# A residual stage of a diffusion backbone: VectorE's work behind the first group's statistics is queued behind the root

## The chip, the cores and the metric

The kernel runs as one program on one core of a Trainium2 chip. The metric is the time of one execution in microseconds (us), the median of several runs. Four engines compute: TensorE (PE, matrix products), VectorE (DVE), ScalarE (ACT) and GpSimd (POOL); SyncE (SP) issues the DMAs. Each engine works through its own queue in order, and they wait for each other by semaphores.

## The reference

Two trunk layers are applied to 640 tokens: 512 latent tokens and 128 context tokens, which share the weights but have their own conditioning vector.

```python
def trunk_layer(x, cond, rope, ctx, layer_idx, ...):
    sh_a, sc_a, g_a, sh_f, sc_f, g_f = modulation(cond, w_mod, b_mod)
    h = rms_norm(x, norm_attn) * (1.0 + sc_a) + sh_a
    proj = h @ w_in
    ...                       # differential attention and grouped-query attention
    mix = jnp.concatenate([out_a, out_b], axis=-1) @ w_out
    x = x + g_a * mix
    h = rms_norm(x, norm_ffn) * (1.0 + sc_f) + sh_f
    gate, up = jnp.split(h @ w_gate_up, 2, axis=-1)
    x = x + g_f * ((jax.nn.silu(gate) * up) @ w_down)
    return x, own_ctx
```

`rms_norm` needs, for each token, the mean of the squares of all 1024 columns and the inverse root of it. So the next normalisation can only be finished when the last column of `x + g * (...)` is there. All values are 32-bit floats.

## The kernel before

The stream `x` is held with its columns in the 128 partitions: eight tiles `x0` to `x7` (`xT`) of 128 columns x 640 tokens (in the order of a built program they are named `x_70` to `x_77`). Every factor of a product is split into a high and a low part, `hi` and `lo` (for weights `whi` and `wlo`): ScalarE writes the high part (L87, or L90 with a bias), VectorE the low one (L88, L91), and `prod` (L710) makes three matmuls of it, high by high (L714), low by high (L715) and high by low (L716). Weights come by DMA into `raw`, and `w_prep` (L687) splits them some tiles ahead of use; `w_next(ahead)` says how many.

Three places close a sub-layer with the norm of the next one behind it, all by `residual` (L1168) with `nxt` given: attention to FFN in layer 0 (boundary 1), FFN of layer 0 to attention of layer 1 (boundary 2), attention to FFN in layer 1 (boundary 3). The first five column blocks go straight through: product into PSUM, `add_gated` (L1161, the gated sum into `x`; one instruction for latent, one for context tokens), `stat_add` (square on ScalarE L363, sum of squares on VectorE L364). For the last three, the tokens are taken in two groups: 256 and 384, or twice 320 at boundary 3. For each group in turn the three products, adds and statistics are made. Then `norm_stats` (L388) turns the sums into one number per token: PE sums over the partitions (L398), VectorE takes the inverse root in twelve small instructions that depend on each other (`rsqrt`, L99 to L105, the last writes `rstd`), and PE spreads `rstd` over the partitions (L402) into a PSUM tile `rb`. `norm_apply` multiplies `x` by the scale and by `rb` (L625, at boundary 3 L450) and splits the result; that is the input of the next products.

The source gives only dependencies and a priority by its order. The compiler's scheduler (`schedule_with_timeline_sim=True`) fixes each engine's queue by its own model of time: whatever it holds to be ready first goes first. So the twelve instructions of the first group's root may stand between instructions of the second group's adds and of the weight splits. PSUM tiles `S` (three of them) hold running products; a product can start when an earlier one's tile has been read.

Of the kernel before, what the change touches and what calls it, by code (L numbers as in the profile page):

```python
# [15 lines left out]
ALU = mybir.AluOpType  # L16
# [4 lines left out]
D = 1024  # L21
KC = D // P
# [24 lines left out]
class Net:  # L47
# [45 lines left out]
    def rsqrt(self, out, src, scale, n):  # L93

        v = self.nc.vector
        a = self.t([P, 32], "rs_a", bufs=2)[:, :n]
        b = self.t([P, 32], "rs_b", bufs=2)[:, :n]
        c = self.t([P, 32], "rs_c", bufs=2)[:, :n]
        v.tensor_scalar(a, src, scale, EPS, ALU.mult, ALU.add)  # L99
        v.tensor_scalar(b.bitcast(I32), a.bitcast(I32), 1, None, ALU.logical_shift_right)  # L100
        v.tensor_scalar(c.bitcast(I32), b.bitcast(I32), -1, 0x5F3759DF, ALU.mult, ALU.add)
        for i in range(3):
            v.scalar_tensor_tensor(b, c, -0.5, a, ALU.mult, ALU.mult)
            v.tensor_tensor(b, b, c, ALU.mult)
            v.scalar_tensor_tensor(out if i == 2 else c, b, 1.5, c, ALU.add, ALU.mult)  # L105


    def setup(self):
# [279 lines left out]
    def norm_stats(self, out, g0, g1):  # L388

        nc = self.nc
        st = self.mm()
        tiles = [(t, min(t, g1 - P)) for t in range(g0, g1, P)]
        n = len(tiles)
        for i, (_, s) in enumerate(tiles):
            nc.tensor.matmul(st[:, i:i + 1], lhsT=self.ssq[:, s:s + P], rhs=self.ones, start=True, stop=True)  # L398
        r = self.t([P, NTILE], "rstd", bufs=2)
        self.rsqrt(r[:, 0:n], st[:, 0:n], 1.0 / D, n)  # L400
        for i, (t, s) in enumerate(tiles):
            nc.tensor.matmul(out[:, t - g0:s + P - g0], lhsT=r[:, i:i + 1].broadcast_to([P, P]),  # L402
                             rhs=self.ident[:, t - s:P], start=True, stop=True)

    def norm_apply(self, state, group, rb):
        if state[1] and state[0] in FAST:
            self.fast_norm(state, group, rb)
            return
        g0, g1 = GROUPS[group]
        for k in range(KC):  # L410
            self.norm_chunk(state, k, g0, g1, rb)
# [756 lines left out]
    def residual(self, l, act, which, order, nxt=None, side=(), steps=1):  # L1168

        if nxt:
            self.stat_begin()
        for mb in range(KC - 3 if nxt else KC):
            w = self.w_next()
            s, parts = self.acc2()
            for i in range(2):
                self.prod(parts[i], self.columns(w, act, GROUPS[i], order))
            self.add_gated(l, which, mb, s, 0, NT)  # L1180
            if nxt:
                self.stat_add(mb, 0, NT)
                if mb == 2:
                    self.warm(AF.Silu if nxt[1] else AF.Exp)
            for _ in range(steps):
                self.step(side)
        if not nxt:
            return None
        while side:
            self.step(side)  # L1190
        state = self.norm_begin(*nxt)
        groups = HALVES if nxt[1] and nxt[0] in FAST else GROUPS
        last = [(mb, self.w_next(), self.acc2(groups)[1]) for mb in (KC - 3, KC - 2, KC - 1)]
        for i, (a, b) in enumerate(groups):
            for mb, w, parts in last:
                self.prod(parts[i], self.columns(w, act, (a, b), order))
                self.add_gated(l, which, mb, parts[i], a, b)
                self.stat_add(mb, a, b)
            rb = self.mm()
            self.norm_stats(rb, a, b)  # L1200
            self.norm_apply(state, i, rb)
        return state[2]

    def ffn(self, l, h, side):
# [135 lines left out]
```

## Time and profile before

| what | value |
|---|---|
| median of 3 runs | 1713.78 us (1711.89 to 1718.52) |
| profiled execution | 1714.41 us, span 1712.6 us |
| mean granted clock of TensorE | 0.984 of full speed |
| PE busy | 1655.6 us, 97% |
| DVE busy | 1173.0 us, 68% |
| ACT busy | 670.4 us, 39% |
| POOL busy | 436.7 us, 25% |

Busy shares are averages over the whole span. Idle time of PE is rare (the chain of work that ended last is 86% PE, 6% DVE, 3% DMA), so the places where PE stands still are worth looking at one by one, in the timeline of each engine. In it a row gives the start and the duration in us, the engine, the line, the operation, the tiles written and read, how many instructions were merged, and in brackets the idle time of the engine just before, with what ended it.

### The profile page before, as it was taken

Reading aid. Unit: us, or ns where it says so; the run is one execution under the profiler, and the core shown is the slowest. Engines: PE = TensorE matmul, PEld = TensorE weight load, DVE = VectorE, ACT = ScalarE, POOL = GpSimd, SP = SyncE. Lnnn points to the kernel's source line nnn. Section 1 sums busy time; section 2 is a strip of 40 time slices with the busy share of each in tenths; the row PEclk is TensorE's granted clock in tenths of the full one; section 3 lists DMA queues with packets and bytes.
Section 4 is the critical chain, followed back from the end, with each engine's and each line's share of the span. In section 5 each row is a group of like instructions: output and inputs, shape, how many; then the busy total and the mean of one; then the engine's idle time right before and its main releaser. Section 6 shows DMA issues by size and latency. Waiting matters only on the chain.

```text
span 1712.6 us, 29412 instructions
## 1 busy us (share of the span) xinstructions
PE 1655.6 (97%) x11958; PEld 1575.6 (92%) x11958; DVE 1173.0 (68%) x2023; ACT 670.4 (39%) x1301; POOL 436.7 (25%) x378
## 2 busy tenths in 40 slices
PE   8989899999999999999999998999999999999999
PEld 6768878898999999999998997888988999999998
DVE  5686768878488988732247885788479944973772
ACT  4433376643422122212235433767335422441440
POOL 0242634410100000000002354444013613641440
PEclk8989999999999999999999999999999999999999
DMA  9343211144155565412122212111311231231222
GB/s 348 120 153 118 56 26 26 50 173 148 50 181 189 177 217 170 151 50 99 56 86 89 83 32 50 26 38 47 115 50 47 77 104 70 74 112 62 74 82 79
DMA packets 44263, 169.22 MB, mean 99 GB/s; under 512 B 5600, under 2 KB 8416, under 8 KB 32864
## 3 DMA queue, kind: packets, MB, share of 16 engines
q1 hardware_dynamic: 44128, 167.34, 29.3%
q8 instruction: 94, 1.54, 0.4%
q14 instruction: 41, 0.34, 0.1%
HBM read 152.90 MB, written 3.93 MB: 92 GB/s over the span
## 4 chain that ended last, share of the span: by engine, by line
PE 86%; DVE 6%; DMA 3%; ACT 2%; POOL 2%; issue 1%; SPq 0%; DVEq 0%; POOLq 0%; ACTq 0%
PE S L715 21%; PE S L714 21%; PE S L716 21%; PE mm L1030 3%; PE S L1009 3%; PE S L925 3%; PE S L926 2%; PE mm L1026 2%; PE S L237 2%; PE mm L714 1%; PE mm L716 1%; PE mm L715 1%; DVE wlo L88 1%; DMA Q<-in_w_mod 1%; DMA raw<-in_w_in 1%
## 5 line engine op out<-in xcount | busy, mean ns | idle before, releaser
L87 ACT ACTIVATE whi<-raw 128x1024 fp32r<-128x1024 f32 (+2 forms) x272 | 225.0, 842 | 618.0 <-PE S L715 518.3
L88 DVE TENSOR_TENSOR wlo<-raw,whi 128x1024 fp32r<-128x1024 f32 (+2 forms) x272 | 293.7, 1093 | 96.6 <-ACT whi L87 92.1
L716 PE MATMUL S<-k,wlo 128*128 128x256 f32 (+2 forms) x904 | 280.1, 310 | 0.0
L714 PE MATMUL S<-k,whi 128*128 128x256 f32 (+2 forms) x904 | 277.7, 311 | 1.6 <-ACT k L90 1.2
L715 PE MATMUL S<-lo,whi 128*128 128x256 f32 (+2 forms) x880 | 272.4, 310 | 0.0
L716 PE MATMUL S<-hi,wlo 128*128 128x384 f32 (+2 forms) x864 | 266.9, 310 | 0.0
L714 PE MATMUL S<-hi,whi 128*128 128x256 f32 (+2 forms) x864 | 266.2, 310 | 0.0
L715 PE MATMUL S<-q,whi 128*128 128x256 f32 (+2 forms) x832 | 258.0, 310 | 0.0
L1161 DVE SCALAR_TENSOR_TENSOR x<-S,modT,x 128x128 f32<-128x128 f32 (+4 forms) x137 | 66.6, 524 | 195.5 <-PE S L716 195.4
L714 PEld LDWEIGHTS S<-k,whi 128*128 128x128 f32 x904 | 170.9, 190 | 3.2 <-ACT k L90 1.4
L716 PEld LDWEIGHTS S<-k,wlo 128*128 128x128 f32 x904 | 172.1, 190 | 0.0
L715 PEld LDWEIGHTS S<-lo,whi 128*128 128x128 f32 x880 | 165.4, 188 | 1.7 <-issue 1.7
L716 PEld LDWEIGHTS S<-hi,wlo 128*128 128x128 f32 x864 | 162.5, 188 | 0.0
L714 PEld LDWEIGHTS S<-hi,whi 128*128 128x128 f32 x864 | 161.7, 188 | 0.8 <-issue 0.8
L715 PEld LDWEIGHTS S<-q,whi 128*128 128x128 f32 x832 | 157.5, 189 | 3.4 <-issue 3.4
L317 DVE SCALAR_TENSOR_TENSOR Q<-V,cT,Q 128x512 f32<-128x512 f32 x224 | 152.6, 745 | 0.0
L714 PE MATMUL S<-whi,hi 128*128 128x256 f32 x512 | 147.1, 288 | 2.4 <-ACT Q L245 1.9
L632 POOL TENSOR_TENSOR lo<-P,hi 128x640 fp32r<-128x640 f32 (+2 forms) x12 | 13.3, 1107 | 533.8 <-ACT hi L631 533.4
L945 DVE TENSOR_REDUCE mx<-S 128x1 f32<-128x768 f32 x128 | 119.5, 951 | 43.4 <-PE S L926 43.1
L716 PE MATMUL S<-whi,lo 128*128 128x256 f32 x512 | 146.2, 286 | 0.2 <-DVE lo L91 0.2
L715 PE MATMUL S<-wlo,hi 128*128 128x256 f32 x512 | 145.7, 285 | 0.0
L714 PEld LDWEIGHTS S<-whi,hi 128*128 128x128 f32 x512 | 97.9, 191 | 5.5 <-issue 2.5
(272 smaller groups left out, 3632.5 us busy)
## 6 DMA issues: line engine op xcount, KB each, us to landing
raw<-in_w_gate_up SPq DMA_DIRECT2D x44, 1024.0 KB, 4.8
V<-in_w_mod SPq DMA_DIRECT2D x64, 512.0 KB, 3.9
raw<-in_w_in SPq DMA_DIRECT2D x16, 1024.0 KB, 4.8
raw<-in_w_down SPq DMA_DIRECT2D x16, 1024.0 KB, 5.0
Q<-in_w_mod SPq DMA_DIRECT2D x32, 256.0 KB, 3.8
raw<-in_w_out SPq DMA_DIRECT2D x8, 1024.0 KB, 4.9
raw<-in_w_down SPq DMA_DIRECT2D x8, 768.0 KB, 4.2
raw<-raw SPq DMA_DIRECT2D x40, 128.0 KB, 2.2
```

Source lines behind the costliest of these rows:

```text
L87: nc.scalar.activation(hi, src, AF.Copy)
L88: nc.vector.tensor_tensor(lo, src, hi.bitcast(F32), ALU.subtract)
L237: nc.tensor.matmul(o, lhsT=l_[k][:, c], rhs=r_[:, w], start=k == 0 and i == 0, stop=k == KC - 1 and i == 2)
L317: ins = nc.vector.scalar_tensor_tensor(a, v, self.cT[:, k, c:c + 1], a, ALU.mult, ALU.add)
L714: self.nc.tensor.matmul(out, lhsT=lh, rhs=rh, start=(i == 0), stop=False)
L715: self.nc.tensor.matmul(out, lhsT=lh, rhs=rl, start=False, stop=False)
L716: self.nc.tensor.matmul(out, lhsT=ll, rhs=rh, start=False, stop=(i == n - 1))
L925: nc.tensor.matmul(out, lhsT=Q[j][:, cols], rhs=keys[:, k0:k0 + n], start=True, stop=False)
L945: nc.vector.tensor_reduce(mx, s[:, 0:n], AX.X, ALU.max, negate=True)
L1009: nc.tensor.transpose(ps[:, i * P:(i + 1) * P], p[:, i * P:(i + 1) * P], self.ident)
L1030: nc.tensor.matmul(o[64 * j:64 * j + 64], lhsT=self.V[:, v, 512 + 64 * j:576 + 64 * j], rhs=pts[j][:, i * P:(i + 1) * P], start=first, sto ...
L1161: self.nc.vector.scalar_tensor_tensor(x[:, s:e], src[:, s - a:e - a], self.m(l, which, mb, c), x[:, s:e], ALU.mult, ALU.add)
```

## The change

`rsqrt` and `norm_stats` return the last instruction of the root. In `residual`, the loop over the two groups is taken apart: the first group is finished, then everything that VectorE gets from `norm_apply` of the first group, from the whole second group (adds, statistics, root) and from one more weight tile is queued behind the last instruction of the first group's root. `issue_after` sets an order in VectorE's queue; it adds no wait for a result. The last `w_next` prepares one tile less ahead, and `w_prep` inside the block makes up for it. In the changed kernel L364 is L365, L398 and L402 are L399 and L403, L450 is L452, L625 is L627 and L1161 is L1163.

```diff
-            v.scalar_tensor_tensor(out if i == 2 else c, b, 1.5, c, ALU.add, ALU.mult)
+            ins = v.scalar_tensor_tensor(out if i == 2 else c, b, 1.5, c, ALU.add, ALU.mult)
+        return ins.ins
...
-        self.rsqrt(r[:, 0:n], st[:, 0:n], 1.0 / D, n)
+        ins = self.rsqrt(r[:, 0:n], st[:, 0:n], 1.0 / D, n)
         for i, (t, s) in enumerate(tiles):
             nc.tensor.matmul(out[:, t - g0:s + P - g0], lhsT=r[:, i:i + 1].broadcast_to([P, P]),
                              rhs=self.ident[:, t - s:P], start=True, stop=True)
+        return ins
...
-        last = [(mb, self.w_next(), self.acc2(groups)[1]) for mb in (KC - 3, KC - 2, KC - 1)]
-        for i, (a, b) in enumerate(groups):
+        last = [(mb, self.w_next(1 if mb == KC - 1 else 2), self.acc2(groups)[1]) for mb in (KC - 3, KC - 2, KC - 1)]
+
+        def finish(i):
+            a, b = groups[i]
             for mb, w, parts in last:
                 self.prod(parts[i], self.columns(w, act, (a, b), order))
                 self.add_gated(l, which, mb, parts[i], a, b)
                 self.stat_add(mb, a, b)
             rb = self.mm()
-            self.norm_stats(rb, a, b)
-            self.norm_apply(state, i, rb)
+            return rb, self.norm_stats(rb, a, b)
+
+
+        rb, chain = finish(0)
+        with self.tc.issue_after(chain):
+            self.norm_apply(state, 0, rb)
+            rb, _ = finish(1)
+            self.w_prep(self.pos + 2)
+        self.norm_apply(state, 1, rb)
         return state[2]
```

What the scheduler makes of it, at boundary 1 on VectorE. `x_75` to `x_77` are the last three column blocks, `PT` the sums of squares, `wlo` a weight's low part, `A` the scale. Before:

```order
L99 TENSOR_SCALAR rs_a<-mm 128x2
L385 SCALAR_TENSOR_TENSOR A<-modT,small 128x8
L88 TENSOR_TENSOR wlo<-raw,whi 128x1024
L385 SCALAR_TENSOR_TENSOR A<-modT,small 128x8
L100 TENSOR_SCALAR rs_b<-rs_a 128x2
L364 TENSOR_TENSOR PT<-PT 128x384
L101 TENSOR_SCALAR rs_c<-rs_b 128x2
...
L105 SCALAR_TENSOR_TENSOR rstd<-rs_b,rs_c 128x2
L625 SCALAR_TENSOR_TENSOR P<-x_70,A,mm 128x256
```

Now, from the start of the root on:

```order
L99 TENSOR_SCALAR rs_a<-mm 128x2
L100 TENSOR_SCALAR rs_b<-rs_a 128x2
L101 TENSOR_SCALAR rs_c<-rs_b 128x2
...
L105 SCALAR_TENSOR_TENSOR rstd<-rs_b,rs_c 128x2
L1163 SCALAR_TENSOR_TENSOR x_75<-S,modT,x_75 128x256
L1163 SCALAR_TENSOR_TENSOR x_75<-S,modT,x_75 128x128
L1163 SCALAR_TENSOR_TENSOR x_76<-S,modT,x_76 128x256
L1163 SCALAR_TENSOR_TENSOR x_76<-S,modT,x_76 128x128
L1163 SCALAR_TENSOR_TENSOR x_77<-S,modT,x_77 128x256
L1163 SCALAR_TENSOR_TENSOR x_77<-S,modT,x_77 128x128
L88 TENSOR_TENSOR wlo<-raw,whi 128x1024 x3
L627 SCALAR_TENSOR_TENSOR P<-x_70,A,mm 128x256
```

The root is in one piece, both scale instructions are ahead of it, and the six adds and three splits, which stood ahead of the root or between its parts, are between it and the first multiplication of `norm_apply`.

At boundary 1 on TensorE, around the second group's broadcast; `k_44..` and `q_44..` are high and low parts of the FFN's input. Before:

```order
L714 MATMUL S<-k_4409,whi 128x256
L402 MATMUL mm<-ident,rstd 128x128 x3
L715 MATMUL S<-q_4417,whi 128x256
L716 MATMUL S<-k_4409,wlo 128x256
L714 MATMUL S<-k_4410,whi 128x256
```

Now:

```order
L717 MATMUL S<-q_4418,whi 128x256
L718 MATMUL S<-k_4410,wlo 128x256
L403 MATMUL mm<-ident,rstd 128x128 x3
L716 MATMUL S<-k_4403,whi 128x384 x3
L717 MATMUL S<-q_4411,whi 128x384
```

The broadcast stood among products of the first group (256 tokens); now it stands behind the last of them and directly ahead of the first product of the second group (384 tokens), which needs it.

At boundary 2 on VectorE, behind the first group's root; `lo_88..` are low parts of the projection's input. Before:

```order
L105 SCALAR_TENSOR_TENSOR rstd<-rs_b,rs_c 128x2
L364 TENSOR_TENSOR PT<-PT 128x384
L625 SCALAR_TENSOR_TENSOR P<-x_70,A,mm 128x256
L625 SCALAR_TENSOR_TENSOR P<-x_71,A,mm 128x256
L625 SCALAR_TENSOR_TENSOR P<-x_72,A,mm 128x256
L99 TENSOR_SCALAR rs_a<-mm 128x3
L91 SCALAR_TENSOR_TENSOR lo_8821<-P,modT,hi_8813 128x256
```

Now:

```order
L88 TENSOR_TENSOR wlo<-raw,whi 128x1024 x2
L365 TENSOR_TENSOR PT<-PT 128x384
L1163 SCALAR_TENSOR_TENSOR x_77<-S,modT,x_77 128x256
L1163 SCALAR_TENSOR_TENSOR x_77<-S,modT,x_77 128x128
L627 SCALAR_TENSOR_TENSOR P<-x_70,A,mm 128x256
L627 SCALAR_TENSOR_TENSOR P<-x_71,A,mm 128x256
L627 SCALAR_TENSOR_TENSOR P<-x_72,A,mm 128x256
L88 TENSOR_TENSOR wlo<-raw,whi 128x1024
L365 TENSOR_TENSOR PT<-PT 128x384
L91 SCALAR_TENSOR_TENSOR lo_8821<-P,modT,hi_8813 128x256
```

Ahead of these rows stand `rstd` and the adds to `x_75` and `x_76`. So two pairs of adds, two splits, a statistics add and a third pair are between `rstd` and the first multiplication, and one more split and statistics add between the multiplications and the first low part.

## Rows read from the trace of the kernel before

**Rows 1.** The page, first part: busy time and share of each engine.
```profile
PE 1655.6 (97%) x11958; PEld 1575.6 (92%) x11958; DVE 1173.0 (68%) x2023; ACT 670.4 (39%) x1301; POOL 436.7 (25%) x378
```

**Rows 2.** PE's waits: who for whom, us in total, times, longest.
```profile
PE mm L402 <- DVE rstd L105: 6.3, 2, 4.0
```

**Rows 3.** Timeline of PE at boundary 1: start, duration, row, idle before.
```profile
421.74 0.92 PE L402 MATMUL mm<-ident,rstd 128*128 128x128 f32 x4 [4.03 <-DVE rstd L105]
422.45 1.28 PE L398 MATMUL mm<-ones,PT 128*128 128x1 f32 x6
423.77 1.00 PE L714 MATMUL S<-k,whi 128*128 128x256 f32 x3
...
431.13 0.83 PE L402 MATMUL mm<-ident,rstd 128*128 128x128 f32 x6
...
435.34 0.69 PE L714 MATMUL S<-k,whi 128*128 128x384 f32 x3
```

**Rows 4.** Timeline of DVE at boundary 1.
```profile
411.56 0.74 DVE L1161 SCALAR_TENSOR_TENSOR x<-S,modT,x 128x256 f32<-128x256 f32 x2 [1.75 <-PE S L716]
412.48 1.23 DVE L88 TENSOR_TENSOR wlo<-raw,whi 128x1024 fp32r<-128x1024 f32 x1 [0.17 <-ACT whi L87]
...
417.78 0.15 DVE L99 TENSOR_SCALAR rs_a<-mm 128x2 f32<-128x2 f32 x1
...
419.87 0.16 DVE L103 SCALAR_TENSOR_TENSOR rs_b<-rs_c,rs_a 128x2 f32<-128x2 f32 x1
...
421.43 0.16 DVE L105 SCALAR_TENSOR_TENSOR rstd<-rs_b,rs_c 128x2 f32<-128x2 f32 x1
422.69 1.26 DVE L625 SCALAR_TENSOR_TENSOR P<-x,A,mm 128x256 f32<-128x256 f32 x3 [1.10 <-PE mm L402]
...
432.08 2.04 DVE L625 SCALAR_TENSOR_TENSOR P<-x,A,mm 128x256 f32<-128x256 f32 x6 [2.20 <-PE mm L402]
434.04 1.14 DVE L91 SCALAR_TENSOR_TENSOR q<-P,modT,k 128x256 fp32r<-128x256 f32 x3
```

**Rows 5.** Timeline of ACT behind boundary 1.
```profile
432.60 0.80 ACT L90 ACTIVATE k<-P,modT 128x256 fp32r<-128x256 f32 x2 [2.81 <-DVE P L625]
...
446.31 1.06 ACT L87 ACTIVATE whi<-raw 128x1024 fp32r<-128x1024 f32 x1 [5.14 <-PE S L715]
447.27 0.68 ACT L1237 ACTIVATE P<-S 128x640 f32<-128x640 f32 x1
```

**Rows 6.** Windows: length; busy PE, PEld, DVE, ACT, POOL; PEclk, DMA share, GB/s.
```profile
423.80:428.80 5.00, 5.00 (x23) 5.00 (x24) 4.97 (x18) 3.81 (x9) 2.01 (x3) 0.50 0.01 2
...
1275.30:1278.50 3.20, 3.20 (x12) 3.20 (x13) 3.06 (x13) 1.13 (x2) 0.00 (x0) 0.51 0.02 5
```

**Rows 7.** Timeline of PE at boundary 2.
```profile
904.46 0.71 PE L402 MATMUL mm<-ident,rstd 128*128 128x128 f32 x4 [2.30 <-DVE rstd L105]
...
906.99 0.58 PE L716 MATMUL S<-whi,lo 128*128 128x256 f32 x1 [0.20 <-DVE lo L91]
```

**Rows 8.** Timeline of DVE at boundary 2.
```profile
897.54 0.55 DVE L364 TENSOR_TENSOR PT<-PT 128x384 f32<-128x384 f32 x1
898.01 0.15 DVE L99 TENSOR_SCALAR rs_a<-mm 128x2 f32<-128x2 f32 x1
...
905.21 1.26 DVE L625 SCALAR_TENSOR_TENSOR P<-x,A,mm 128x256 f32<-128x256 f32 x3 [0.34 <-PE mm L402]
...
906.46 0.48 DVE L91 SCALAR_TENSOR_TENSOR lo<-P,modT,hi 128x256 fp32r<-128x256 f32 x1
```

**Rows 9.** Timeline of PE at boundary 3.
```profile
1273.66 0.42 PE L715 MATMUL S<-k,whi 128*128 128x320 f32 x1 [1.10 <-DVE k L91]
...
1275.28 0.57 PE L715 MATMUL S<-k,whi 128*128 128x320 f32 x1 [0.47 <-DVE k L91]
...
1280.15 0.78 PE L402 MATMUL mm<-ident,rstd 128*128 128x128 f32 x6
```

**Rows 10.** Timeline of DVE at boundary 3.
```profile
1272.17 0.97 DVE L100 TENSOR_SCALAR rs_b<-rs_a 128x3 int32<-128x3 int32 x1
```

## The prediction

> **What bounds the kernel now.** The page's first part comes first: TensorE (PE) is busy 97% of the span [rows 1], so a microsecond counts only where PE stands still, or runs at its lower clock. The view of PE's waits comes next: the longest wait for VectorE (DVE) in the whole kernel is that of the broadcast at L402 for `rstd`, 6.3 us in two places [rows 2]. The timeline then puts these at the two boundaries of layer 0: 4.03 us before 421.74 (boundary 1, attention to FFN) [rows 3] and 2.30 us before 904.46 (boundary 2, FFN to layer 1) [rows 7]. At boundary 3 (layer 1, attention to FFN) there is no such row; PE reaches L402 there without waiting for the root. The reader is to see in rows 3 and 4 what ends the stop: the root's twelve instructions run from 417.78 to 421.43+0.16, L402 follows at 421.74, DVE takes its result at 422.69, and PE's first product starts at 423.77, 1.08 us after that. After it the clock is at 0.50 for 5 us [rows 6].
>
> **Boundary 1, part by part.** *The root.* Undisturbed it needs 0.195 us a step (419.87 to 421.43 is eight steps) [rows 4], so twelve instructions last 11 x 0.195 + 0.16 = 2.3 us instead of 3.8, because a split of weights and a statistics add leave it. One small scale instruction now stands before it (+0.1). So `rstd` ends at 417.78 + 0.1 + 2.3 = 420.2, 1.4 us earlier, and L402 with it.
>
> *What the root displaced.* The order shows what now stands between `rstd` and the first L627 (L625 before): the gated adds of the last three column blocks and the low halves of three weight tiles. Before, all adds and two splits ran from 407 on, in time in which DVE waited for PE (1.75 us of idle before 411.56 alone) [rows 4]; now they run after 420.2. A pair of adds takes 0.74 and a split 1.23, each less the 0.08 by which neighbours overlap: 3 x 0.66 + 3 x 1.15 = 5.4 us. The first L627 starts at 425.6 instead of 422.69: **+2.9**. The cover is only the 1.10 us in which DVE waited for L402 anyway [rows 4], and it is in this sum. PE's first product follows 1.08 later, at 426.7.
>
> *The statistics of the second group.* Their L398 took 1.28 us in the stop, between 422.45 and 423.77 [rows 3]. Now it stands among products, because the adds and squares that it needs are late. At full clock I take 0.7 for it, and 0.3 for the first low half (L91), which has a statistics add more before it: **+1.0**.
>
> *The second broadcast.* Before, L402 of the second group was issued at 431.13 in the middle of first-group products, and PE worked on these until the second group's first product at 435.34 [rows 3]; DVE (432.08) and ScalarE (432.60) made that group's input meanwhile [rows 4, 5]. In the new order L403 stands behind all products of the first group. PE then has nothing: from L402's start to the first high half ready it is 432.60 + 0.80 - 431.13 = 2.27 us, of which L402 itself fills 0.7, so 1.6 stand open; the first low half (434.04 + 0.75) comes 1.4 us after that, of which the three products that need the high half alone fill 0.5. **+2.5**.
>
> *The next accumulator.* The three running products now end within 1 us of each other, and the fourth needs the bank of the first. ScalarE puts a split of 1.06 before the Silu of 0.68 that frees it [rows 5]; 1.7 less that 1 us of work: **+0.9**, the slack of the last term being read off the new order, so 0 to 1.7.
>
> *The clock.* The stop before the first product is now 5.8 us in place of 4.03 (and the 1.28 in which only L398 ran), and a second one of 2.5 us is added. After the first, PE again runs at the lower clock (0.50) for a stretch; I take the same cost as before. For the second, boundary 3 gives the nearest rows: stops of 1.10 and 0.47 us before 1273.66 and 1275.28 [rows 9] were followed by 3.2 us at 0.51 [rows 6], in which half the speed costs 1.6 us: **+1.6**, bounds 0 and 5 (both stretches twice as long).
>
> The Trainium skill (TensorE: Matmul & The Clock Gate, section "Why this matters for your kernels") warns that an idle gap between bursts of matmuls puts the array back to half rate. The rows agree that a stop is followed by 0.50, and by that rule this change, which makes a longer stop and one more, would lose at the clock again, as the last term has it; without the rule's second fall the sum below would be 1.6 less.
>
> Boundary 1 together: 2.9 + 1.0 + 2.5 + 0.9 + 1.6 = **8.9 us** (5 to 13).
>
> **Boundary 2.** The root starts at 898.01 at the latest and lasts 2.3, so `rstd` is there at 900.3, while PE has products until 904.46 - 2.30 = 902.16: PE's wait for the root is gone, 2.3 us. But DVE has two pairs of adds, two splits, a statistics add (0.55 less 0.08) and the third pair to do first [rows 4, 8]: 900.3 + 3 x 0.66 + 2 x 1.15 + 0.5 = 905.0, against 905.21 for the first L625. So the first product gains 0.2. Then the third split and another add (1.15 + 0.5) stand before the first L91, which was at 906.46 and comes at 905.0 + 3 x 0.4 + 1.6 = 907.8; PE waited for that L91 already, before 906.99 [rows 7], and now does so 1.3 us longer. The second group's L398 adds 0.4 to it, half of what it took among products above, as PE also waited in places there. **+1.7** (0 to 3).
>
> **Boundary 3.** The root already lay beside products; nothing is gained. The first L91 moves by a few tenths. The second group's root, until now interleaved with L450 and L91, is queued behind them as a block; one of its instructions also ran long (L100 0.97, where a step of the root is 0.195) [rows 10]. It ends about 0.3 us after 1280.15, where L402 started without a wait [rows 9], and PE, whose input came no later, stands still before it in one piece (some 2.9 us) and not in two (1.10 and 0.47 before). I take 0.3 and 1.3 for a lower clock after it, from the 1.6 above: **+1.6** (0 to 3.5).
>
> GpSimd's work shared that time. The Trainium skill (SBUF — State Buffer, section "Who interferes with whom") says that a GpSimd instruction and a VectorE one that takes the shared port pair exclude each other; the long L100 fits it. By it the block of twelve, if it meets GpSimd's instructions as they start later, could lose another 2 us, and the sum would be 14; otherwise it stays.
>
> **Sum.** 8.9 + 1.7 + 1.6 = 12.2 us on the profiled execution of 1714.41: 1726.6. That execution is 0.6 above the median of the runs shown (1713.78), so the median to expect is **1726**. The other small shifts of the order (in layer 1's projection and attention) I take at nothing: the same instructions stand there a place or two apart, beside PE's work; uncovered they could be half a microsecond either way. Bounds added up: 5 + 0 + 0 to 13 + 3 + 3.5, that is 1719 to 1733.
>
> **Rivals.** *No change (within 0.5%, 1705 to 1722).* The second stop is covered and the fourth accumulator comes in time, so boundary 1 pays only 2.9 + 1.0, boundary 2 1.3 and boundary 3 0.3: 5.5 us, 1719. For it: terms of 2.5 and 0.9 rest on the place of L403 in a queue, and on products that PE at half clock would do more slowly, giving DVE time. Against: L403 stands behind all of them, however slow they are. *Faster.* What the root no longer waits for decides, and the displaced work fits in the time of L402: boundary 1 gains 1.4 and boundary 2 2.3, and with shorter stops the clock stays up, worth at most 2.5 (half of 5 us at 0.50) and 2.8 more: 9 us, 1705. For it: `rstd` is what the view of waits names. It decides if less than 1.1 us of DVE work stands between `rstd` and L627; the order has 5.4 and 4.7 there, so hardly. *It doesn't do what it says* is excluded by the order: the root stands as one block at all three places.
>
> **Chances.** Forecast (slower by 12, beyond 0.5%): 0.80. No change: 0.17. Faster: 0.03. 0.5%, 8.6 us, is about what a measurement of this kernel can tell from no change. The range 1718 to 1733 holds the forecast's bounds and the upper part of the second case.
>
> **What would show it.** Right: at boundary 1, `rstd` near 420.2, the first L627 near 425.6, PE's first product near 426.7, a new stop of 2 to 3 us right behind the second group's L403 and the second group's first product near 440; at boundary 2, L403 near 902 without a wait for `rstd`, and the first L91 near 907.8. Wrong: if the first product at boundary 1 comes before 424, the displaced work was not on the path; if the second stop is missing, the sum is too high by 2.5 to 4.

## The result and the profile after

The changed kernel takes 1727.19 us (median of six runs, 1725.16 to 1730.47) against 1713.34 (1709.44 to 1718.52) of the kernel before: the ratio is 1.0085, with a 95% interval of 1.0071 to 1.0099. It is slower by 12 to 17 us; 1726 had been forecast. The profiled execution lasts 1727.22, with a span of 1725.3. The first part of the page, beside [rows 1]: PE has as much to do as before, and the span is 12.7 us longer.

```profile
PE 1655.9 (96%) x11958; PEld 1575.9 (91%) x11958; DVE 1177.6 (68%) x2023; ACT 671.6 (39%) x1301; POOL 438.6 (25%) x378
```

PE's waits in the changed kernel (for whom; us in total, times, longest), beside [rows 2]. In the new program the three matmuls of `prod` are L716 to L718; in e4, e7 and e9 further down some lines have moved by one more.

```profile
PE S L716 <- ACT k L90: 7.7, 3, 5.0
...
PE S L883 <- DVE Q L859: 5.3, 3, 2.4
...
PE S L716 <- ACT hi L90: 3.6, 2, 3.1
...
PE mm L403 <- DVE rstd L105: 3.2, 2, 2.5
```

The wait for `rstd` has fallen from 6.3 to 3.2 us, as the change intends. In its place stand waits of the first products for their input (k and hi), which the kernel before did not show with such lengths.

Boundary 1 on PE, which answers to [rows 3] (start, duration, row, idle before):

```profile
418.30 0.50 PE L399 MATMUL mm<-ones,PT 128*128 128x1 f32 x4
421.33 1.17 PE L403 MATMUL mm<-ident,rstd 128*128 128x128 f32 x4 [2.53 <-DVE rstd L105]
427.52 1.01 PE L716 MATMUL S<-k,whi 128*128 128x256 f32 x3 [5.03 <-ACT k L90]
434.06 0.72 PE L399 MATMUL mm<-ones,PT 128*128 128x1 f32 x6
438.86 0.83 PE L403 MATMUL mm<-ident,rstd 128*128 128x128 f32 x6
441.17 0.79 PE L716 MATMUL S<-k,whi 128*128 128x384 f32 x3 [1.49 <-ACT k L90]
442.56 0.44 PE L717 MATMUL S<-q,whi 128*128 128x384 f32 x1 [0.59 <-DVE q L91]
...
455.51 0.38 PE L716 MATMUL S<-k,whi 128*128 128x256 f32 x1 [0.70 <-ACT P L1248]
```

And on DVE, which answers to [rows 4]:

```profile
421.02 0.16 DVE L105 SCALAR_TENSOR_TENSOR rstd<-rs_b,rs_c 128x2 f32<-128x2 f32 x1
421.10 2.04 DVE L1163 SCALAR_TENSOR_TENSOR x<-S,modT,x 128x256 f32<-128x256 f32 x6
423.05 3.49 DVE L88 TENSOR_TENSOR wlo<-raw,whi 128x1024 fp32r<-128x1024 f32 x3
426.45 1.26 DVE L627 SCALAR_TENSOR_TENSOR P<-x,A,mm 128x256 f32<-128x256 f32 x3
```

This execution came to the boundary 1.09 us later than that of before, by chance (the program up to there is unchanged). With that taken off, `rstd` starts at 419.93 and not at 421.43, but between it and the first multiplication lie 5.4 us of adds and splits. The multiplication starts at 425.36 in place of 422.69, PE's first product at 426.43 in place of 423.77. Behind the second broadcast (438.86) PE stands still twice, for 1.49 and 0.59 us; it had worked on there before.

Boundary 2 on PE and DVE, beside [rows 7] and [rows 8] (this execution is 7.50 us later here):

```profile
909.50 0.61 PE L403 MATMUL mm<-ident,rstd 128*128 128x128 f32 x4
913.25 0.58 PE L716 MATMUL S<-whi,hi 128*128 128x256 f32 x1 [3.14 <-ACT hi L90]
915.95 0.58 PE L718 MATMUL S<-whi,lo 128*128 128x256 f32 x1 [1.91 <-DVE lo L91]
...
917.70 1.41 PE L399 MATMUL mm<-ones,PT 128*128 128x1 f32 x6
...
926.83 0.39 PE L716 MATMUL S<-whi,hi 128*128 128x256 f32 x1 [0.48 <-ACT hi L90]
```

```profile
912.18 1.26 DVE L627 SCALAR_TENSOR_TENSOR P<-x,A,mm 128x256 f32<-128x256 f32 x3
...
914.95 1.34 DVE L91 SCALAR_TENSOR_TENSOR lo<-P,modT,hi 128x256 fp32r<-128x256 f32 x2
```

Where the time went can be read by pairing each product of PE with the same product in the first trace of before and watching how the difference of their starts grows. It grows in five places; the columns are the differences over each stretch, in us, for the traces of all experiments below (b. 1 is boundary 1).

```
                            start   b. 1   b. 2  projection  attention  b. 3   all
changed kernel               1.1    6.4    2.5     2.3         1.3      -0.9   12.7
changed again (e10)         -0.4    6.3    2.5     2.3         1.2      -1.0   11.0
before again (e11)          -0.4   -0.5   -0.3    -0.2         0.4      -1.2   -2.1
e1 boundary 1 only           1.8    8.4    0.0    -0.2        -1.0      -0.9    8.1
e2 boundary 2 only           1.8   -0.4    2.7     2.3         1.4      -0.9    6.9
e3 boundary 3 only           1.6   -0.7   -0.5    -0.2        -0.5      -1.2   -1.3
e4 statistics early         -1.1    2.2    0.1     2.3         0.3       1.1    4.8
e5 adds only                 0.0    2.8   -0.1     0.0         0.3      -1.1    2.0
e6 splits only               0.2    0.5   -0.3     0.2        -0.4      -1.0   -0.7
e7 multiplications first     1.4    9.4   -0.1     0.1         0.2      -1.1    9.8
e8 b. 2, head root whole    -1.8    0.0    3.1     1.1         1.7      -0.9    3.1
e9 second broadcast ahead   -0.5    5.7   -0.4    -0.2        -0.4      -1.1    3.1
e12 products in the stop     2.3   -1.2   -0.3     0.1        -0.6      -1.2   -0.9
```

The first column is chance alone, up to four us between executions of the same instructions, and single traces have to be held against it. So have those rows of the other columns in which the order was the old one: they lie between -0.7 and 0.0 at boundary 1, and between -1.0 and 0.4 in the attention.

### The profile page after: what moved, and what is told of

The parts are those of the page before. It is cut to its first block, busy times and chain, and to the rows that moved or that the text cites. A ratio compares the mean times of both kernels' runs of the same rounds, so it can differ in the third digit from the quotient of the medians.

```text
span 1725.3 us, 29404 instructions
## 1 busy us (share of the span) xinstructions
PE 1655.9 (96%) x11958; PEld 1575.9 (91%) x11958; DVE 1177.6 (68%) x2023; ACT 671.6 (39%) x1301; POOL 438.6 (25%) x378
## 5 line engine op out<-in xcount | busy, mean ns | idle before, releaser
L716 PE MATMUL S<-k,whi 128*128 128x256 f32 (+2 forms) x904 | 277.3, 310 | 8.6 <-ACT k L90 7.7
L718 PE MATMUL S<-k,wlo 128*128 128x256 f32 (+2 forms) x904 | 278.7, 309 | 0.0
L718 PE MATMUL S<-hi,wlo 128*128 128x384 f32 (+2 forms) x864 | 267.0, 310 | 0.0
L716 PE MATMUL S<-hi,whi 128*128 128x256 f32 (+2 forms) x864 | 266.2, 310 | 0.0
L1163 DVE SCALAR_TENSOR_TENSOR x<-S,modT,x 128x128 f32<-128x128 f32 (+4 forms) x137 | 66.2, 525 | 186.4 <-PE S L718 186.2
L716 PEld LDWEIGHTS S<-k,whi 128*128 128x128 f32 x904 | 170.3, 189 | 10.8 <-ACT k L90 8.4
L718 PEld LDWEIGHTS S<-k,wlo 128*128 128x128 f32 x904 | 170.7, 189 | 0.0
L718 PEld LDWEIGHTS S<-hi,wlo 128*128 128x128 f32 x864 | 162.5, 188 | 0.0
L716 PEld LDWEIGHTS S<-hi,whi 128*128 128x128 f32 x864 | 161.7, 188 | 0.8 <-issue 0.8
L716 PE MATMUL S<-whi,hi 128*128 128x256 f32 x512 | 148.4, 290 | 5.7 <-ACT hi L90 3.6
L634 POOL TENSOR_TENSOR lo<-P,hi 128x640 fp32r<-128x640 f32 (+2 forms) x12 | 13.9, 1162 | 536.8 <-ACT hi L633 534.3
L718 PE MATMUL S<-whi,lo 128*128 128x256 f32 x512 | 146.6, 287 | 1.9 <-DVE lo L91 1.9
L716 PEld LDWEIGHTS S<-whi,hi 128*128 128x128 f32 x512 | 99.3, 194 | 9.1 <-ACT hi L90 4.0
```

The source lines that it names most:

```text
L716: self.nc.tensor.matmul(out, lhsT=lh, rhs=rh, start=(i == 0), stop=False)
L718: self.nc.tensor.matmul(out, lhsT=ll, rhs=rh, start=False, stop=(i == n - 1))
L1163: self.nc.vector.scalar_tensor_tensor(x[:, s:e], src[:, s - a:e - a], self.m(l, which, mb, c), x[:, s:e], ALU.mult, ALU.add)
```

## The experiments

Each experiment edits the part of `residual` behind `norm_begin`, or one other place. Their runs of the kernel before have medians of 1713.65 (e1 to e4), 1713.44 (e5 to e8) and 1713.52 (e9 to e12). Each of these three sets ran on a chip of its own, so versions of different sets are compared with care.

### One boundary at a time

The whole new block of `residual` is used at one boundary, the old loop at the others (e2 has `(1, 0)` in the condition, e3 `(1, 1)`):

```
+        if nxt == (0, 1):
             last = [(mb, self.w_next(1 if mb == KC - 1 else 2), self.acc2(groups)[1]) for mb in (KC - 3, KC - 2, KC - 1)]
...
+        else:
+            last = [(mb, self.w_next(), self.acc2(groups)[1]) for mb in (KC - 3, KC - 2, KC - 1)]
+            for i, (a, b) in enumerate(groups):
...
```

> The change at boundary 1 alone (attention of layer 0 to its FFN); boundaries 2 and 3 as in the kernel before. Theory A (each boundary pays for what its own order does): the two traces put 6.4 us of the 12.7 at boundary 1, so about 1713.3 + 6.4 = 1720, no stretch behind it moves against the kernel before, and the products of the second group start with a stop of about 2 us behind the second broadcast. Theory B (the prediction's sizes): 1713.3 + 8.9 = 1722. Rival C (the stretch of layer 1's projection and attention, 3.6 us in the trace of the changed kernel, comes from one run to the next or from being later): it is there here too, about 1723 to 1724.

Measured: 1721.73, ratio 1.0050 (1.0034 to 1.0066). The interval, 5.8 to 11.3 us, holds the times of all three theories; the trace decides. Nothing is lost in layer 1, so rival C fails, and the loss there is not a consequence of being late. Boundary 1 cost 8.4 us in this trace, and not the 6.4 that Theory A took from the first; e10 explains the difference.

> The change at boundary 2 alone (FFN of layer 0 to layer 1). Theory A: 2.5 us at the boundary and 3.6 in layer 1's projection and attention, whose order on VectorE this change alone brings (a split of weights inside the first head root, GpSimd's products 14 us later, beside the next root): about 1719.5, and the root's scale and shift instructions behind the heads' reductions last 1.3 us instead of 0.2. Theory B (the prediction's sizes, projection at nothing): 1713.3 + 1.7 = 1715. Rival C (the projection's loss is chance): 1715 to 1716, with no longer waits of PE for Q than before.

Measured: 1718.96, ratio 1.0038 (1.0023 to 1.0053), and in the trace 2.7 us at the boundary, 2.3 in the projection, 1.4 in the attention. Theory A holds: the order at boundary 2 alone brings the loss further on.

> The change at boundary 3 alone (attention of layer 1 to its FFN). Theory A (read from the traces): PE has the second group's root in one block that ends no later, and one stop less before its second group: 0.9 us gained, about 1712.4. Theory B (the prediction): 1.6 us lost, 1715. No difference from 1713.3 that can be measured would leave both open; the stretch of the trace between the last products of the attention's residual and the first FFN unit decides then.

Measured: 1713.16, ratio 0.9997 (0.9986 to 1.0008). By the time neither theory is told from no change; the trace gives -1.2, but so do all traces with the old order at boundary 3. The change is worth nothing here. By the medians the three single changes add up to 12.9 us (8.1, 5.3 and -0.5), against 13.9 for all of them together.

### The changed kernel and the kernel before once more

No edit; one execution each (1725.49 and 1712.32).

> The changed kernel once more, for a second trace. Boundary 1 cost 6.4 us in its first trace and 8.4 in that of the change at boundary 1 alone, with the same orders there. If that is chance between executions, this trace lies between or beside them (6 to 8.5); boundary 2 again 2.5 to 2.7, layer 1's projection 2.3, attention 1.4, boundary 3 as in the other traces.

> The kernel before once more, for a second trace. All traces since the first lose about 1 us less at boundary 3 than the first trace of the kernel before, also those with the same order there. If the first trace had 1 us of chance at boundary 3 (GpSimd meeting VectorE's instructions), this one shows the stretch 0.9 to 1.1 us shorter, and the change at boundary 3 is worth nothing; if it shows it as long as the first, the orders behind boundary 2 shorten it.

Boundary 1 costs 6.3 again, and the other places are near what was expected. What e1 had on top is the clock (a granted clock of 1.00 is 2.4 GHz, 0.5 is 1.2 GHz). The windows that begin 3.5 us behind the first product and right behind the second stop, first of the changed kernel, then of e1 (length; busy PE, PEld, DVE, ACT, POOL; PEclk, DMA share, GB/s):

```profile
431.00:434.10 3.10, 3.10 (x27) 3.10 (x26) 1.95 (x5) 2.19 (x6) 1.96 (x3) 0.90 0.44 177
...
442.90:446.00 3.10, 3.10 (x20) 3.10 (x19) 3.10 (x8) 2.63 (x8) 1.92 (x2) 1.00 0.00 0
```

```profile
431.70:435.20 3.50, 3.50 (x25) 3.50 (x25) 1.94 (x5) 2.18 (x6) 2.09 (x3) 0.75 0.38 154
...
444.10:447.20 3.10, 3.10 (x11) 3.10 (x11) 3.10 (x9) 2.62 (x8) 1.91 (x2) 0.52 0.00 0
```

The order is the same, and so are the stops before it. Behind the second stop PE gets 20 products done in one and 11 in the other; that is 1.5 of the 2.0 us. The other 0.5 came behind the first stop, where e1's low clock reaches some 1 us further into the products. At boundary 3 it is the same story with the kernel before. In its second trace the stops of [rows 9] are there to the hundredth, but the stretch behind them, which ran at 0.51 in [rows 6], has the full clock:

```profile
1272.71 0.42 PE L715 MATMUL S<-k,whi 128*128 128x320 f32 x1 [1.10 <-DVE k L91]
...
1274.33 0.42 PE L715 MATMUL S<-k,whi 128*128 128x320 f32 x1 [0.47 <-DVE k L91]
```

```profile
1274.40:1277.50 3.10, 3.10 (x20) 2.88 (x21) 2.96 (x13) 1.13 (x2) 0.00 (x0) 1.00 0.02 5
```

It is 1.2 us shorter for that. My guess in the expectation, that GpSimd was the cause, is wrong: the long L100 is there as before (0.98). So the first trace of before, from which the prediction was made, happened to have a low clock at boundary 3, and the change loses or gains nothing there (-0.9 and -1.0 against -1.2).

### Adds, splits, and their place

At boundary 1 alone, e5 takes `w_prep` out of the block that is held back and prepares the tiles as before; e6 leaves only `w_prep` in it. First e5, then e6, each against e1:

```
-            last = [(mb, self.w_next(1 if mb == KC - 1 else 2), self.acc2(groups)[1]) for mb in (KC - 3, KC - 2, KC - 1)]
+            last = [(mb, self.w_next(), self.acc2(groups)[1]) for mb in (KC - 3, KC - 2, KC - 1)]
...
-                self.w_prep(self.pos + 2)
```

```
+            self.norm_apply(state, 0, rb)
+            rb, _ = finish(1)
             with self.tc.issue_after(chain):
-                self.norm_apply(state, 0, rb)
-                rb, _ = finish(1)
                 self.w_prep(self.pos + 2)
```

> Boundary 1 alone, and there only the second group's products, gated adds and statistics are held back behind the root; the three weight splits are prepared as in the kernel before. Order of VectorE: one split still lies in the root, the six adds lie between the root and the first multiplication; order of PE: the second group's broadcast behind all products of the first group. Theory A (what stands between the root and the first multiplication costs its time, and the broadcast behind all products costs a stop): root 0.7 to 1.4 us later than with everything held, adds 2.0 us, so the first multiplication about 0.5 to 1 us later than in the kernel before, then the second group's statistics among products (1.0), a stop of about 2 us and its clock: 4.5 to 6 us, 1718 to 1719.5. Rival (the splits are what costs, the adds fit in the wait for the broadcast): 1 us, 1714.5.

> Boundary 1 alone, and there only the preparation of weight tiles is held back behind the root; the second group's adds and statistics are as in the kernel before, and the second broadcast stands ahead of the last 26 products of the first group in PE's queue. Theory A: the splits (3.4 us) put the first multiplication 1.4 to 2 us later than in the kernel before, there is no second stop: 1.5 to 3 us, 1715 to 1716.5. Rival (the splits make up most of the 8 us that boundary 1 costs, since the stop before the first product and the clock behind it follow from them): 5 to 6 us, 1719.

Measured: 1717.28, ratio 1.0034 (1.0021 to 1.0048), and 1717.08, ratio 1.0015 (1.0002 to 1.0028). In the traces boundary 1 costs 2.8 and 0.5. PE with the adds only, then with the splits only:

```profile
424.10 1.01 PE L716 MATMUL S<-k,whi 128*128 128x256 f32 x3 [1.60 <-ACT k L90]
...
437.48 0.79 PE L716 MATMUL S<-k,whi 128*128 128x384 f32 x3 [1.48 <-ACT k L90]
```

```profile
425.11 1.01 PE L716 MATMUL S<-k,whi 128*128 128x256 f32 x3 [2.50 <-ACT k L90]
...
431.97 0.83 PE L403 MATMUL mm<-ident,rstd 128*128 128x128 f32 x6
```

With the adds only, the first product is 0.3 us late and the second stop is there (1.48): it follows from the adds, which make the second group's statistics late and so put its broadcast behind all products. With the splits only, the first product is 1.2 us late (with the chance ahead of the boundary taken off, as everywhere), there is no second stop, and 0.6 of it is caught up later. Neither half accounts for the whole, and the rivals of both fail by the traces. Theory A holds in kind in both, but its sizes (4.5 to 6 and 1.5 to 3) are above what the traces show. The two halves together make 3.3 and not 6.4. Of the rest, 1.2 is missing at the first product already (0.3 and 1.2 against 2.7): each half alone has as cover the 1.10 us in which DVE waits for the broadcast [rows 4], and both together have it only once. That is an argument, and what else is missing was not followed. The times alone bound the two shares less well: the intervals are 3.6 to 8.2 us for the adds and 0.3 to 4.8 for the splits.

In e7 the root is followed by all eight multiplications of the first group, and only these by the rest:

```
+                muls = self.norm_apply(state, 0, rb)
+            with self.tc.issue_after(muls[7] if muls else chain):
                 rb, _ = finish(1)
                 self.w_prep(self.pos + 2)
```

> Boundary 1 alone: the root in one block, then all eight multiplications of the first group, and only behind these the second group's adds, its statistics and the splits. Rival (the place decides: only what stands ahead of the first multiplication costs): the first product comes 1.3 us earlier than in the kernel before, at 422.5 on its clock, and the loss of 8 us shrinks to the second stop of about 2 us and its clock: 1715 to 1717. Theory A' (the amount decides: the 5.4 us that VectorE had done in its idle time ahead of the root must be done before the second group's first product, wherever they stand): the first product comes 1.3 us early, then the second group's statistics, root and broadcast come late, one stop of 6 us or more lies ahead of the second group's products, and the loss is as large as with the change alone or larger: 1721 to 1725.

Measured: 1724.09, ratio 1.0063 (1.0051 to 1.0075); 9.4 us at boundary 1. The rival fails. The time lies in the band of Theory A', but that is luck in part: by it the first product was to come early and one long stop to follow, and the first product came late. DVE and PE:

```profile
422.80 1.26 DVE L626 SCALAR_TENSOR_TENSOR P<-x,A,mm 128x256 f32<-128x256 f32 x3 [1.27 <-PE mm L403]
...
427.81 2.03 DVE L1163 SCALAR_TENSOR_TENSOR x<-S,modT,x 128x256 f32<-128x256 f32 x6
```

```profile
428.69 0.55 PE L716 MATMUL S<-k,whi 128*128 128x256 f32 x1 [5.93 <-DVE x L1163]
```

With the 1.43 us of chance in this execution taken off, the multiplications start at 421.4, 1.3 earlier than in the kernel before, and yet the first product comes only at 427.3: it waits for an add. All three accumulators (`S`, `bufs=3`) hold the last column blocks of the residual until the second group's adds have read them, so the adds free the tile that the first FFN product writes. In the kernel before they had been done in time, ahead of the root. PE then waits 1.59 us for the second group's `rstd` and 1.49 behind its broadcast. So the adds can't stand behind the multiplications. Whether the splits alone could (root, adds, multiplications, then splits) was not run.

### The second broadcast

The change at boundary 1 alone, with DVE's order as it is there, and the third FFN unit's first-group products behind the second broadcast in PE's queue:

```
 ffn:   for i in range(2):
+           with self.tc.issue_after(self.cast) if (l, pi, j, u, i) == (0, 0, 1, 0, 0) else nullcontext():
                self.prod(parts[i], self.columns(w, h, GROUPS[i], range(KC)))
```

> The change at boundary 1 alone (1721.73 by itself, +8.1), and the first group's products of the third FFN unit stand behind the second group's broadcast in PE's queue, so that the broadcast has 24 products behind it instead of none; VectorE's order at the boundary is the same, word for word. Theory A (the place of the second broadcast is a term of its own): PE reaches the broadcast about 2.7 us earlier, waits about 1 us for its root, the 24 products cover its way through VectorE and ScalarE, the stop of 1.5 and 0.6 us ahead of the second group is gone: about 2 us gained, 1719.5 to 1720. Rival (the second group's input is late because its root is late, wherever the broadcast stands): the stop only moves ahead of the broadcast, 1721 to 1722.

Measured: 1719.16, ratio 1.0038 (1.0020 to 1.0056), 2.6 us less than e1, though the intervals overlap and e1 ran on another chip. In the trace the stops of 1.49 and 0.59 us are gone and one of 0.52 has come ahead of the broadcast:

```profile
433.04 0.72 PE L400 MATMUL mm<-ones,PT 128*128 128x1 f32 x6
436.28 0.91 PE L404 MATMUL mm<-ident,rstd 128*128 128x128 f32 x6 [0.52 <-DVE rstd L106]
```

Theory A holds in kind: the stops go with the place of the broadcast. How much that is worth stays open. Boundary 1 costs 5.7 us in this trace, against 8.4 in e1 but 6.4 and 6.3 in the two traces of the changed kernel; the low clock behind the first stop reached further in e9 (0.59 from 429.40 to 433.00, beside the 0.90 of the changed kernel shown above), which hides part of what was gained.

### The loss in layer 1

The prediction took the shifts of order there at nothing. In the first head block's root, the changed kernel has on DVE (two splits, two reductions and waits for ScalarE lie between the first two rows, which are 6.3 us apart):

```profile
944.47 0.18 DVE L99 TENSOR_SCALAR rs_a<-ss 128x20 f32<-128x20 f32 x1
...
950.74 0.17 DVE L105 SCALAR_TENSOR_TENSOR rq<-rs_b,rs_c 128x20 f32<-128x20 f32 x1
...
951.15 1.55 DVE L847 TENSOR_TENSOR Q<-Q,rq 128x640 f32<-128x640 f32 x2
952.62 1.32 DVE L99 TENSOR_SCALAR rs_a<-ss 128x20 f32<-128x20 f32 x1
```

and on POOL and PE:

```profile
952.10 4.16 POOL L849 TENSOR_TENSOR Q<-Q,small 128x640 f32<-128x640 f32 x2 [15.45 <-ACT whi L87]
```

```profile
966.76 0.74 PE L883 MATMUL S<-ident,Q 128*128 128x128 f32 x5 [1.87 <-DVE Q L859]
```

In the kernel before, with one split and one reduction in it, the same root lasted 4.2 us, and GpSimd began 14 us earlier:

```profile
932.69 0.18 DVE L99 TENSOR_SCALAR rs_a<-ss 128x20 f32<-128x20 f32 x1
...
936.69 0.18 DVE L105 SCALAR_TENSOR_TENSOR rq<-rs_b,rs_c 128x20 f32<-128x20 f32 x1
```

```profile
937.87 4.18 POOL L847 TENSOR_TENSOR Q<-Q,small 128x640 f32<-128x640 f32 x2 [13.26 <-ACT Q L793]
```

Of the 14 us the boundaries explain 10; 4 are new. The next root then stands beside GpSimd's first block from its start; its steps take up to 1.32 us, where the longest had been 0.71, and PE waits 1.87 for Q, where it had no wait. For the test, the change at boundary 2 alone (e2) and the first head root traced ahead of the second block, whose DVE work is held back:

```
 project:
+            if l == 1 and i == 1:
+                with self.tc.issue_after(self.project_post(l, *done.pop())):
+                    done = [self.project_block(l, h, self.blocks[i], False, [])]
+                continue
```

> The change at boundary 2 alone (1718.96 by itself, +5.3), and in layer 1's projection the first head block's root is traced ahead of the second block, whose work on VectorE is held back behind it. Theory A (the 3.7 us lost in the projection come from the split and the reductions that the new order puts inside the first head root: GpSimd's products start 14 us later than before, beside VectorE's next root, whose steps take 0.66 to 1.3 us there instead of 0.2): the root lasts 2.5 us instead of 6.4, GpSimd starts about 4 us earlier, most of the 3.7 us come back: 1715 to 1716.5. Rival (the loss is the later arrival of data after the boundary, or chance): it stays at 1718 to 1720.

Measured: 1716.94, ratio 1.0024 (1.0016 to 1.0033), 2.0 us less than e2, though the intervals overlap and e2 ran on another chip. The root lasts 2.5 us and PE's wait for Q is gone; a wait of 1.04 for a key tile has come. The projection costs 1.1 in place of 2.3, where traces with the old order lie within 0.2 of nothing. So half of this loss is shown to come from the root that was taken apart. The 1.2 to 1.7 us in the attention stay and were not followed; by the spread of the table there, some of it can be chance.

### Versions that might have been faster

e4 leaves DVE alone and changes PE's queue: the second group's products of the second to last block stand behind the first group's statistics, those of the last block behind its broadcast.

```
+        rb, *_ = finish(1, (None, sums, cast))
...
+            for (mb, w, parts), ins in zip(last, behind):
+            with self.tc.issue_after(ins) if ins is not None else nullcontext():
                 self.prod(parts[i], self.columns(w, act, (a, b), order))
```

> No work of VectorE is held back. Instead PE's queue is changed at all three boundaries: the second group's products of the second to last column block stand behind the first group's statistics, and those of the last block behind the first group's broadcast. Theory A (the stop at boundary 1 comes from the statistics' place in PE's queue, behind all products of the second group, not from what interleaves with the root): the root runs beside 4 us of products, the broadcast waits for nothing or for under 1 us, the first product follows the last product of the residual without a stop; 6.5 us (417.2 to 423.8 in the trace of before) less the 2 to 3 us of a stop that stays at the second group's broadcast, and about 3 us at boundary 2: 1705 to 1708. Rival D (VectorE's work is the bound at the boundaries, wherever the root stands): the second group's adds and splits, now among the first group's multiplications, hold up PE by as much: 1712 to 1716.

Measured: 1719.07, ratio 1.0037 (1.0024 to 1.0051): Theory A fails, and so does the band of rival D.

```profile
409.33 0.66 PE L343 MATMUL mm<-ident,P 128*128 128x128 f32 x4 [2.17 <-DVE P L340]
409.82 0.50 PE L400 MATMUL mm<-ones,PT 128*128 128x1 f32 x4
416.02 0.61 PE L404 MATMUL mm<-ident,rstd 128*128 128x128 f32 x4
...
433.13 0.79 PE L717 MATMUL S<-k,whi 128*128 128x384 f32 x3 [1.49 <-ACT k L91]
```

The broadcast indeed waits for nothing, and the first product starts 2.0 us earlier than before (420.67, with 1.14 of chance). But PE waits 2.17 for the sums of the modulation that stand ahead of the statistics, the second stop is there again (1.49), and the order in the projection moves here too (2.3).

e12 is the kernel before with ten products more in the stop at boundary 1:

```
+        with self.tc.issue_after(last.ins):
+            for w, x in fill:
+                nc.tensor.matmul(out[:, 0:512], lhsT=w, rhs=x, start=True, stop=True)
```

> The kernel before, with ten more products of 512 columns (2.1 us at full clock) between the first group's statistics and its broadcast at boundary 1, written to the tile that the broadcast overwrites; they compute nothing that is used. They fill half of the 4.03 us in which PE waits for the root. Theory C (the low clock behind the stop, 0.50 for 5 us, is a term of its own): the clock behind the broadcast stays higher, up to 2.5 us are gained, 1711 to 1712. Rival (what remains of the stop, some 3 us, lowers the clock as well, or the first products wait for VectorE anyway): 1713 to 1714, with the granted clock of the 5 us behind the first product near 0.5, or near 1 without gain.

Measured: 1713.45, ratio 0.9999 (0.9990 to 1.0008). The clock does stay up, which beats the rival's first half, and no gain can be measured, as its second half says; the interval leaves room for 1.7 us, and the trace has -1.2 at boundary 1, where the old order has -0.7 to 0.0. The window behind the first product, which ran at 0.50 in [rows 6]:

```profile
426.20:429.00 2.80, 2.66 (x18) 2.35 (x19) 2.80 (x10) 2.07 (x7) 1.20 (x2) 1.00 0.91 325
```

DVE is busy for all 2.80 us of it. That fits first products that are fed at DVE's pace, with which PE at half clock had kept up; it is not shown further. No version was faster than the kernel before.

## Why the prediction was right, and where its sum was not

**Right: the mechanism at boundaries 1 and 2.** Each event that the prediction named as a sign of being right came, with 1.09 taken off at boundary 1: `rstd` ready at 420.1 (420.2 predicted), first L627 at 425.4 (425.6), first product at 426.4 (426.7), a new stop right behind the second broadcast, second group's first product at 440.1 ("near 440"). At boundary 2, with 7.50 off, L403 at 902.0 without a wait (902) and the first L91 at 907.5 (907.8). The displaced work was on the path.

**Boundary 1, terms.** Pairing the FFN's products in their order, with 1.09 taken off, gives the terms one by one. Displaced work: 2.7 (2.9 predicted). First low half 0.4 and L399 among products 0.7 (1.0 together). Second broadcast: 2.6 (2.5), of which the stops are 1.49 + 0.59; e9 bears out that they come from its place. Accumulator: 0.7 (0.9), the row at 455.51. From this 0.6 goes off, because the low clock behind the first stop reached only 4.1 us into the products and not 5.1; the prediction had it cost the same. But for rounding, that makes the 6.4 us found. The step that failed is the clock behind the second stop, "**+1.6**, bounds 0 and 5": the stop was followed by 1.00 in both traces of the changed kernel and by 0.52 in e1. It is worth 0 or 1.5, by chance. The Trainium skill (TensorE: Matmul & The Clock Gate, section "Why this matters for your kernels") warns that an idle gap between bursts of matmuls puts the array back to half rate. Its row is about longer gaps than these two, so the prediction was wrong to apply it to the second stop. The traces agree with it for the stop of 4.03 us [rows 3], with 0.50 behind it [rows 6].

**Boundary 2, terms mis-sized.** 2.5 to 2.7 (1.7 predicted, within 0 to 3). The first product came 0.5 earlier and the first L91 1.0 later, as predicted within 0.4. The statistics of the second group, taken at 0.4, last 1.41 at the lower clock (917.70), and the paired products fall back by 1.4 over them. The second broadcast was not in the sum: six matmuls of the first group stand behind it where it had been 27, and it leaves a stop of 0.48 (926.83). Nor was a longer time at the lower clock behind the stops of 3.14 and 1.91: in the window that begins 9.5 us behind the start of the broadcast the changed kernel is still at 0.50, the kernel before at 1.00. The windows, of the changed kernel and of before:

```profile
919.00:922.00 3.00, 3.00 (x15) 3.00 (x16) 2.72 (x12) 1.33 (x3) 1.47 (x2) 0.50 0.00 0
```

```profile
910.00:914.00 4.00, 3.99 (x19) 3.44 (x18) 2.27 (x9) 1.95 (x5) 1.45 (x2) 0.55 0.02 4
914.00:918.00 4.00, 4.00 (x36) 4.00 (x35) 3.98 (x12) 3.46 (x10) 1.05 (x1) 1.00 0.00 0
```

These costs come to more than 2.5 together, as the kernel before paid some of them at other places. No experiment isolated them.

**Boundary 3, wrong.** The stop of "some 2.9 us" in one piece, from which the term starts, didn't come; the changed kernel waits 0.65 us there:

```profile
1292.77 0.85 PE L403 MATMUL mm<-ident,rstd 128*128 128x128 f32 x6 [0.65 <-DVE rstd L105]
```

"I take 0.3 and 1.3 for a lower clock after it" gave 1.6; e3 and e11 show nothing. The kernel before had the low clock in the trace that was read, so it could only go up.

**Layer 1, wrong.** "The other small shifts of the order ... I take at nothing" cost 3.5 to 3.6 us, more than the half microsecond allowed. The order had been compared, the places were known, and the rule that one instruction in a root delays everything behind it, which the prediction used at boundary 1, was not applied to the head roots. The Trainium skill (SBUF — State Buffer, section "Who interferes with whom") says that a GpSimd instruction and a VectorE one that takes the shared port pair exclude each other. The prediction brought it up at boundary 3, where nothing was lost; in the projection the row at 952.62 (1.32 beside GpSimd's 4.16) fits it.

So 12.2 was predicted and 12.7 found in the trace (13.9 by the medians), but two clock terms (2.9 together) were too much and stood in for most of the layer 1 loss of 3.5 to 3.6. That the total came out so close is luck in part: boundary 1 was sized well but for the clock, the other parts were not. The rivals fail clearly: no change needed the second stop to be covered, faster needed less than 1.1 us of displaced work.

## What to carry to other kernels

A chain of small instructions that is kept whole pushes the work between its steps behind it, and that work had been done in idle time; before doing so, sum what will stand between the chain's end and the first instruction that waits for it, and look for the accumulators that this work frees. A hold on one engine can change the order far from it (here the head root in layer 1, behind boundary 2): read the order far behind the edit for the same pattern, a chain with a long instruction put inside it. And repeat a trace before a term of one or two microseconds is read from it.

## What the runs showed of the hardware

After stops of 0.5 to 1.5 us in an otherwise full stretch, the granted clock was 1.00 in some executions and 0.51 or 0.52 over some 3 us in others, with the same instructions in the same order (boundary 3 of the kernel before, the second stop of boundary 1); that was worth 1.2 us at the one place and 1.5 at the other. Where VectorE was busy all the time (4.97 of 5.00 us [rows 6]), 5 us at 0.50 cost too little to be measured by the times (e12, under 1.7 us). Steps of a root on 128x20 elements, 0.18 us by themselves, took up to 1.32 beside GpSimd's multiplications of 128x640.
